# Moving the start addresses of four weight buffers in a two-layer encoder kernel

## The chip, the core and the metric

The kernel runs on one core of one Trainium2 chip. The metric is device microseconds (us) of the whole program. TensorE (PE in the profile) multiplies matrices: a weight load (PEld) puts a 128x128 stationary operand into the array, and a matmul streams a moving operand of up to 512 columns through it into PSUM. VectorE (DVE), ScalarE (ACT) and GpSimd (POOL) work on SBUF and PSUM, and DMA queues move data between HBM and SBUF.

## The reference

Two encoder layers work on 256 tokens of width 1024, in float32:

```python
for l in range(DEPTH):          # DEPTH = 2
    x = mixer_sublayer(x, norm1_g[l], w_in[l], ..., w_out[l], tables)
    x = channel_sublayer(x, norm2_g[l], w_gate_up[l], conv_w[l], conv_b[l], w_down[l])
...
def channel_sublayer(x, n2, w_gu, cw, cb, w_dn):
    h = rms_norm(x, n2)
    g, u = jnp.split(h @ w_gu, 2, axis=-1)
    g = depthwise_conv_centred(g, cw, cb)
    return x + (jax.nn.gelu(g, approximate=False) * u) @ w_dn
```

The mixer projects the normed input to 2560 columns, runs three kinds of attention on 16 heads of width 64 (a neighbourhood, a dilated and a grouped one), norms each kind's output, and projects back to 1024. The channel part widens to 2 x 2816 columns and comes back to 1024.

## The kernel before

**Precision by splitting.** Every large product is made of operands that are split in two: a rounded part ("hi") and what the rounding left ("lo"), both in a 4-byte float type that TensorE takes at one column a cycle. A product is then three matmuls, hi by hi, hi by lo and lo by hi (`mm3`, lines 708 to 711). In the gate and up products (`half_up`, lines 1337 to 1372) the weights are the stationary operand and the activations, hi and lo side by side in one tile `hT`, are the moving one: eight matmuls of 512 columns with the weights' hi part ("wide" below), then eight of 256 columns with their lo part ("narrow"), and that twice for a unit of 256 weight columns. In the projections, the output projections and the down product (`down`, lines 1424 to 1444), the weights are the moving operand, 384, 256 or 512 columns at a time.

**The weight buffers.** All weights pass through the pool `wp` in units of up to 2048 columns (8 KB a partition). A DMA on SP's queue loads a unit into one of four `raw` buffers (`load`, lines 644 to 674). ACT copies it, rounded, into one of two `hi` buffers, and DVE writes raw minus hi into one of two `lo` buffers, 384 to 1024 columns an instruction (`split`, lines 676 to 695). Units take the two slots of each kind in turn. The split runs two units ahead of the matmuls (`AHEAD`, line 42). The output projection's weights of layer 1 are split early, during layer 0, and parked in HBM (`keep`, lines 628 to 642); four of those six units come back by DMA from POOL's queue straight into hi and lo buffers (lines 687 to 689), the other two into buffers of the pool `act`.

**The order of the work.** Every call is first recorded. A planner (`Plan.order`, lines 323 to 465) puts the instructions of all engines in one order from a table of costs, and `emit` (lines 467 to 472) issues them in that order; therefore all instructions carry line 472 in the profile, and groups are told apart by the names of their tiles. In the feed-forward part, one step is a gate unit, a down unit and an up unit: 64 matmuls of the gate and up products and 24 of the down product, 22 steps in the two layers.

**Where buffers get their address.** `Slots.place` (lines 175 to 181) asks the real pool for one tile per slot when the slot is first used, and `View.bind` (lines 146 to 163) cuts the operand of an instruction out of it. The planner doesn't see addresses. In the built program of before, all tiles of `wp` and all large ones of `act` begin at a multiple of 512 bytes in each partition (hi 0 at 69632, lo 0 at 77824, hi 1 at 102400, lo 1 at 110592). Within them, matmul operands begin at multiples of 512 bytes, too. Two kinds of tiles differ: `const_x`, the residual stream, begins 384 bytes past a multiple of 512; and in the value tiles `const_v` (line 598, rows of 13 or 5 heads of 256 bytes) every second weight load begins 256 bytes past one.

Of the kernel before, what the change touches and what calls it, by code (L numbers as in the profile page):

```python
# [37 lines left out]
BANK = 512  # L38
# [124 lines left out]
        return ap  # L163


class Slots:


# [6 lines left out]
    def place(self, t):  # L175
        if t.slot not in self.places:
            shape = list(t.shape) if self.dram else [P, BANK if self.psum else self.cols]
            self.places[t.slot] = self.pool.real.tile(
                shape, self.dtype, tag=f"{self.tag}{t.slot}", name=f"{self.pool.name}_{self.tag}{t.slot}", bufs=1
            )  # L180
        return self.places[t.slot]


# [55 lines left out]
class Plan:  # L239
# [83 lines left out]
    def order(self):  # L323
# [79 lines left out]
        while len(done) < len(ops):  # L403
# [24 lines left out]
            for t in o.tiles:  # L428
                if t.slot is None:
                    s = t.pool  # L430
                    s.given += 1
                    place = min(s.free)
                    s.free.remove(place)
                    t.since, t.slot = taken_at(place[0], ""), place[1]
# [1117 lines left out]
```

## Time and profile before

| what | value |
|---|---|
| time, median of 3 runs | 605.19 us (604.93 to 605.29) |
| the profiled execution's own time | 605.52 us |
| its span, first to last instruction | 603.7 us |
| PE busy, PEld busy | 598.0 us (99%), 526.5 us (87%) |
| DVE, ACT, POOL busy | 485.0, 428.6, 81.0 us |
| granted TensorE clock | 1.00 all along, the 2.4 GHz level |
| DMA | 121.44 MB, mean 201 GB/s |

A matmul's bar in the trace overlaps the next one's, as matmuls are pipelined and their ends modelled. What a matmul costs is the distance from its start to the next one's start, and "pace" below means that distance.

### The profile page before, as it was taken

How to read it: one execution, taken by the hardware profiler on the slowest of the kernel's cores; microseconds unless marked ns; L12 is line 12 of the kernel's file. 1: busy time of each engine (PE TensorE's matmuls, PEld its weight loads, DVE VectorE, ACT ScalarE, POOL GpSimd, SP SyncE). 2: the span in 40 equal slices, each digit the busy share in tenths (PEclk: the TensorE clock that was granted, in tenths of full speed). 3: DMA queues.
4: the chain of work that ended last, by engine and by line, in shares of the span. 5: the costliest groups of instructions: out<-in, count | busy, mean ns of one | idle time of the engine just before them, and what ended most of it. 6: DMA issues, size and time to landing. Idle time of an engine off the chain costs nothing.

```text
span 603.7 us, 9899 instructions
## 1 busy us (share of the span) xinstructions
PE 598.0 (99%) x3496; PEld 526.5 (87%) x3496; DVE 485.0 (80%) x995; ACT 428.6 (71%) x1065; POOL 81.0 (13%) x130
## 2 busy tenths in 40 slices
PE   8999999999999999999999999999999999999997
PEld 7999898888888888888899989888888888888886
DVE  4899988997788988888777898777977777777775
ACT  6889999696566767666688899676766556665661
POOL 2733030102400000000023214421000000000000
PEclk9999999999999999999999999999999999999999
DMA  8993313567588898989454726844465556555601
GB/s 281 292 334 108 106 36 108 181 202 241 174 239 295 280 347 301 331 291 318 153 148 157 254 71 244 280 177 140 140 208 203 171 186 210 175 178 206 197 12 69
DMA packets 85217, 121.44 MB, mean 201 GB/s; under 512 B 9880, under 2 KB 69880, under 8 KB 85168
## 3 DMA queue, kind: packets, MB, share of 16 engines
q1 hardware_dynamic: 82896, 112.17, 55.9%
q0 software_dynamic: 1728, 8.39, 4.1%
q8 instruction: 27, 0.44, 0.3%
q10 hardware_dynamic: 544, 0.26, 0.2%
q14 instruction: 22, 0.18, 0.1%
HBM read 110.93 MB, written 9.88 MB: 200 GB/s over the span
## 4 chain that ended last, share of the span: by engine, by line
PE 97%; ACT 1%; DVE 1%; POOL 0%; issue 0%; DVEq 0%; POOLq 0%
PE psw_w L472 53%; PE psa_a L472 44%; ACT act_s2k L472 0%; POOL small_rstd L472 0%; ACT act_z L472 0%; DVE act_z L472 0%; ACT act_hT L472 0%; DVE wp_lo L472 0%; DVE act_sw L472 0%; POOL small_ms L472 0%; DVE const_x L472 0%; DVE act_qo L472 0%; ACT wp_hi L472 0%; POOL const_warm L472 0%; DVEq L472 0%
## 5 line engine op out<-in xcount | busy, mean ns | idle before, releaser
L472 DVE TENSOR_TENSOR wp_lo<-wp_raw,wp_hi 128x512 fp32r<-128x512 f32 (+2 forms) x332 | 231.4, 731 | 57.2 <-ACT wp_hi L472 40.3
L472 ACT CAST wp_hi<-wp_raw 128x512 fp32r<-128x512 f32 (+2 forms) x332 | 203.0, 663 | 21.6 <-PE psw_w L472 10.1
L472 PE MATMUL psw_w<-act_hT,wp_hi 128*128 128x512 f32 x704 | 179.8, 393 | 0.0
L472 PEld LDWEIGHTS psw_w<-act_hT,wp_hi 128*128 128x128 f32 x704 | 127.8, 189 | 24.2 <-DVE act_hT L472 0.6
L472 PE MATMUL psa_a<-wp_hi,act_hT 128*128 128x384 f32 (+2 forms) x448 | 112.9, 332 | 0.7 <-ACT wp_hi L472 0.7
L472 PEld LDWEIGHTS psw_w<-act_hT,wp_lo 128*128 128x128 f32 x704 | 97.7, 190 | 6.7
L472 PE MATMUL psw_w<-act_hT,wp_lo 128*128 128x256 f32 x704 | 102.2, 282 | 0.0
L472 PEld LDWEIGHTS psa_a<-wp_hi,act_hT 128*128 128x128 f32 x448 | 78.4, 189 | 3.3 <-ACT wp_hi L472 0.9
L472 PE MATMUL psa_a<-wp_lo,act_hT 128*128 128x384 f32 (+2 forms) x224 | 74.4, 334 | 0.1
L472 ACT COPY act_s2k<-psw_w 128x256 f32<-128x256 f32 x88 | 32.4, 372 | 59.4 <-PE psw_w L472 58.9
L472 PE MATMUL psa_a<-wp_lo,act_ch 128*128 128x512 f32 (+1 forms) x176 | 68.3, 388 | 0.0
L472 PE MATMUL psa_a<-wp_hi,act_ch 128*128 128x512 f32 x176 | 68.2, 388 | 0.0
L472 PE MATMUL psa_a<-wp_hi,act_cl 128*128 128x512 f32 (+1 forms) x176 | 67.5, 387 | 0.0
L472 DVE TENSOR_TENSOR act_s2k<-psw_w,act_s2k 128x256 f32<-128x256 f32 x88 | 36.6, 421 | 12.8 <-ACT act_s2k L472 12.0
L472 PEld LDWEIGHTS psa_a<-wp_lo,act_hT 128*128 128x128 f32 x224 | 42.3, 189 | 2.4 <-DVE wp_lo L472 1.1
L472 PEld LDWEIGHTS psa_a<-wp_hi,act_cl 128*128 128x128 f32 x176 | 33.1, 188 | 6.8
L472 PEld LDWEIGHTS psa_a<-wp_hi,act_ch 128*128 128x128 f32 x176 | 33.1, 188 | 6.3
L472 PEld LDWEIGHTS psa_a<-wp_lo,act_ch 128*128 128x128 f32 x176 | 33.1, 188 | 6.0
L472 DVE SCALAR_TENSOR_TENSOR act_s2k<-act_s2k,act_cw,act_s2k 128x255 f32<-128x255 f32 x88 | 36.8, 477 | 1.4 <-ACT act_s2k L472 1.3
L472 ACT ACTIVATE act_s2k<-act_s2k 128x512 f32<-128x512 f32 x22 | 13.9, 632 | 30.3 <-DVE act_s2k L472 30.2
L472 ACT ACTIVATE act_s2k<-act_s2k,act_cw 128x256 f32<-128x256 f32 x44 | 24.1, 596 | 15.3 <-DVE act_s2k L472 15.3
L472 POOL TENSOR_TENSOR small_rstd<-small_ms,const_mh 128x6 f32<-128x6 f32 (+2 forms) x26 | 30.9, 1188 | 14.2 <-DVE small_ms L472 12.6
(132 smaller groups left out, 792.0 us busy)
## 6 DMA issues: line engine op xcount, KB each, us to landing
wp_raw<-in_w_gate_up_dram SPq DMA_DIRECT2D x44, 1024.0 KB, 4.9
wp_raw<-in_w_down_dram SPq DMA_DIRECT2D x22, 1024.0 KB, 7.2
wp_raw<-in_w_in_dram SPq DMA_DIRECT2D x14, 768.0 KB, 5.2
wp_raw<-in_w_in_dram SPq DMA_DIRECT2D x8, 1024.0 KB, 6.8
wp_raw<-in_w_out_dram SPq DMA_DIRECT2D x8, 768.0 KB, 9.3
dram_khi<-act_mixT_hi SPq DMA_DIRECT2D x4, 768.0 KB, 3.6
dram_klo<-act_mixT_lo SPq DMA_DIRECT2D x4, 768.0 KB, 8.3
wp_lo<-dram_klo POOLq DMA_DIRECT2D x4, 768.0 KB, 4.7
```

The costliest lines, as they stand in the source:

```text
L472: getattr(o.engine.real, o.method)(*map(real, o.args), **{k: real(v) for k, v in o.kw.items()})
```

## The change

Four weight buffers, the two hi and the two lo slots of `wp`, get 128 more columns (512 bytes) each, and the part of them that is used begins 8, 48, 16 or 32 columns in, that is 32 bytes (hi 0), 192 (hi 1), 64 (lo 0) and 128 (lo 1). All instructions, their order and their sizes stay. Tiles that lie behind one of the four move up by 512 bytes for each, 2048 in all, so they keep their place relative to a multiple of 512. The raw buffers stay on multiples of 512.

```diff
+SHIFTS = {("hi", 0): 8, ("hi", 1): 48, ("lo", 0): 16, ("lo", 1): 32}
+
+
 class Slots:
...
     def place(self, t):
         if t.slot not in self.places:
             shape = list(t.shape) if self.dram else [P, BANK if self.psum else self.cols]
-            self.places[t.slot] = self.pool.real.tile(
+            shift = SHIFTS.get((self.tag, t.slot), 0)
+            if shift:
+                shape[1] += BANK // 4
+            place = self.pool.real.tile(
                 shape, self.dtype, tag=f"{self.tag}{t.slot}", name=f"{self.pool.name}_{self.tag}{t.slot}", bufs=1
             )
+            self.places[t.slot] = place[:, shift:] if shift else place
         return self.places[t.slot]
```

## Rows read from the trace of the kernel before

**Rows 1.** The page: busy time of PE and PEld, and the chain that ended last.

```profile
PE 598.0 (99%) x3496; PEld 526.5 (87%) x3496; DVE 485.0 (80%) x995; ACT 428.6 (71%) x1065; POOL 81.0 (13%) x130
...
PE 97%; ACT 1%; DVE 1%; POOL 0%; issue 0%; DVEq 0%; POOLq 0%
```

**Rows 2.** Waits of PE: who waited for whom, us, times, longest us.

```profile
PE psw_w L472 <- POOL const_warm L472: 1.0, 1, 1.0
PE psa_a L472 <- ACT wp_hi L472: 0.7, 1, 0.7
```

**Rows 3.** Groups of PE on the weight buffers: count, busy us, mean ns, idle us.

```profile
L472 PE MATMUL psw_w<-act_hT,wp_hi 128*128 128x512 f32 x704 | 179.8, 393 | 0.0
L472 PE MATMUL psa_a<-wp_hi,act_hT 128*128 128x384 f32 (+2 forms) x448 | 112.9, 332 | 0.7 <-ACT wp_hi L472 0.7
L472 PE MATMUL psw_w<-act_hT,wp_lo 128*128 128x256 f32 x704 | 102.2, 282 | 0.0
L472 PE MATMUL psa_a<-wp_lo,act_hT 128*128 128x384 f32 (+2 forms) x224 | 74.4, 334 | 0.1
L472 PE MATMUL psa_a<-wp_lo,act_ch 128*128 128x512 f32 (+1 forms) x176 | 68.3, 388 | 0.0
L472 PE MATMUL psa_a<-wp_hi,act_ch 128*128 128x512 f32 x176 | 68.2, 388 | 0.0
L472 PE MATMUL psa_a<-wp_hi,act_cl 128*128 128x512 f32 (+1 forms) x176 | 67.5, 387 | 0.0
```

**Rows 4.** Timeline of PE, 237.8 to 249 us: start us, us until its end, instruction.

```profile
237.81 0.40 PE L472 MATMUL psa_a<-wp_hi,act_ch 128*128 128x512 f32 x1
...
238.97 0.39 PE L472 MATMUL psa_a<-wp_hi,act_cl 128*128 128x512 f32 x1
...
243.05 0.39 PE L472 MATMUL psa_a<-wp_hi,act_cl 128*128 128x512 f32 x1
243.28 1.98 PE L472 MATMUL psw_w<-act_hT,wp_hi 128*128 128x512 f32 x8
245.09 1.12 PE L472 MATMUL psw_w<-act_hT,wp_lo 128*128 128x256 f32 x8
246.04 2.00 PE L472 MATMUL psw_w<-act_hT,wp_hi 128*128 128x512 f32 x8
247.88 1.12 PE L472 MATMUL psw_w<-act_hT,wp_lo 128*128 128x256 f32 x8
```

**Rows 5.** The chain in order of time, one step: start us, us, what.

```profile
226.82 11.15 PE psw_w L472 x64
237.97 5.47 PE psa_a L472 x24
```

**Rows 6.** Views by tile: duration ns min/median/max of matmuls whose stationary tile differs.

```profile
L472 PE MATMUL psw_w<-const_ident,const_x x64: 270/272/421, 4.7 to 417.7; 128*128 128x128 f32 x64
L472 PE MATMUL psw_w<-const_ident,act_z x60: 270/272/273, 28.6 to 379.4; 128*128 128x128 f32 x60
...
L472 PE MATMUL psw_w<-act_ch,const_v x128: 274/282/387, 55.0 to 404.8; 128*128 128x256 f32 x128
L472 PE MATMUL psw_w<-act_hT,wp_lo x704: 274/283/287, 120.4 to 588.4; 128*128 128x256 f32 x176
```

**Rows 7.** Groups of DVE and ACT that fill the buffers, from the page.

```profile
L472 DVE TENSOR_TENSOR wp_lo<-wp_raw,wp_hi 128x512 fp32r<-128x512 f32 (+2 forms) x332 | 231.4, 731 | 57.2 <-ACT wp_hi L472 40.3
L472 ACT CAST wp_hi<-wp_raw 128x512 fp32r<-128x512 f32 (+2 forms) x332 | 203.0, 663 | 21.6 <-PE psw_w L472 10.1
```

**Rows 8.** Stretch 138 to 300 us: PE, PEld, DVE, ACT, POOL busy, clock, DMA.

```profile
138.00:300.00 162.00, 162.00 (x857) 139.67 (x856) 133.79 (x227) 106.57 (x195) 11.10 (x18) 1.00 0.81 273
```

**Rows 9.** DMA issues into the moved buffers: KB each, median us to landing.

```profile
wp_lo<-dram_klo POOLq DMA_DIRECT2D x4, 768.0 KB, 4.7
wp_hi<-dram_khi POOLq DMA_DIRECT2D x4, 768.0 KB, 5.9
```

## The prediction

> **What bounds the kernel now.** I read the page first: PE is busy for 598.0 of 603.7 us, and 97% of the chain that ended last lies on PE [rows 1]. The view of PE's waits confirms it: in the whole execution PE waits twice, 1.7 us together [rows 2]. No transfer and no other engine is waited for. The time is thus the sum of the matmuls' paces, and the change can move it by two ways alone: it changes the pace of matmuls that read the moved buffers, or it slows those that fill them by so much that PE begins to wait.
>
> How many matmuls read them is in PE's groups: 704 + 448 + 704 + 224 + 3 x 176 = 2608 with hi or lo weights on either side [rows 3] (the output projections, not shown, add to that). One TensorE cycle at the granted 2.4 GHz is 0.42 ns, so **one cycle on each is 1.1 us**, 0.18% of the time. About 0.2%, 1.2 us, is what a measurement of this kernel can tell from no change. The question is whether a start address is worth a cycle or more.
>
> The timeline shows the paces. In a down unit, 18 matmuls of 512 columns take from 238.97 to 243.05 us, 0.2267 us each; but the five before them, of the same shape and from the same buffers, take 0.232 (237.81 to 238.97) [rows 4]. The up and gate products show the same: eight wide matmuls that follow wide ones take 1.81 us (243.28 to 245.09), eight that follow narrow ones 1.84 (246.04 to 247.88) [rows 4]. Nothing is waited for there. After each change of width PE thus needs some matmuls to settle. And the settled pace is not the ideal one: 512 columns at 2.4 GHz are 213.3 ns, so 13.3 ns of each go elsewhere. PE and PEld are busy at the same time for most of the span [rows 1]: the next weights are read from SBUF while the moving operand streams. If the two reads got into each other's way, both the 13.3 ns and the settling could hang on addresses. That is the only place where I can see this change act.
>
> **The change, part by part.** *Instructions and waits*: none is added, removed or moved, and no queue is passed. Each part is costed at nothing but the following.
>
> *Weights as stationary operand* (1408 matmuls on the gate and up products). No row shows a weight load that begins 32, 64, 128 or 192 bytes past a multiple of 512. The nearest do so at other places. Transposes of const_x, which begins 384 bytes past, have the same shortest and median duration as transposes of act_z, which begins on a multiple: 270 and 272 ns [rows 6]. In the attention's last product every second weight load of const_v begins 256 bytes past a multiple; shortest and median are 274 and 282 ns, against 274 and 283 for the lo weights, all of which begin on one [rows 6]. So two other starts cost nothing that shows. I take 0, from these rows.
>
> *Weights as moving operand* (1200 of the 2608). No row has a moving operand off a multiple of 512. Both ends have to come from the paces. **Below**: the shift undoes the settling. In one step that is 0.03 us for the down unit (5.47 us against 24 x 0.2267 = 5.44 [rows 4, 5]) and 0.03 for each of the three of four wide blocks that follow narrow ones, 0.12 us in all. 22 steps make 2.6 us. The steps are 22 x (11.15 + 5.47) = 366 us of the span [rows 5]; if the rest has as much, it is 2.6 x 603.7/366 = 4.3 us. **Above**: matmuls that read a moved buffer never settle, and pay 0.232 for 0.2267 us, 5 ns. Hi 0 alone begins off a multiple of 64 bytes; hi buffers serve 704 + 448 + 352 = 1504 matmuls [rows 3], of which hi 0 has half, and 752 x 5 ns = 3.8 us. Between -4.3 and +3.8 us I take 0: the nearest rows, those of the shifted weight loads, are at 0.
>
> Here a row and a rule differ. The row is that equal matmuls without a wait have two paces [rows 4]. The Trainium skill, SBUF — State Buffer, section "Who interferes with whom", says that PE reads the moving operand and the weights through two independent ports, and that PE and ACT never wait on anyone. By that rule neither pace can hang on an address, and the sum stays at 0; it leaves the two paces without an explanation, so it isn't proof. By the row taken as a collision of the reads, the sum could be -2.6 us.
>
> *Writes by ACT and DVE into the buffers*. 332 instructions each, 663 and 731 ns on average [rows 7]. From 138 to 300 us, DVE is busy 133.79 of 162 us and ACT 106.57 [rows 8]. DVE's 28.2 idle us over that stretch's 9.7 steps with 10 pieces each, 97 pieces, leave 0.29 us a piece, 40% of its duration: so much slower would each have to be before DVE sets the pace. If that cover went, each 0.1 us beyond it would cost 22 x 10 x 0.1 = 22 us. I see no reason for such a slowdown and cost it at nothing.
>
> *The eight DMAs into hi and lo*. They take 4.7 and 5.9 us [rows 9], and no wait of PE is for a transfer [rows 2]. A start 32 bytes off may cost them something; PE's work on the units before them hides it. Nothing.
>
> The sum is 0. The profiled execution took 605.52 us, its span of 603.7 and 1.8 around it; that is 0.33 over the median of 605.19, to which the forecast refers: **605.2 us**.
>
> **The rivals.** *Faster, the settling goes.* If the two paces come from weight load and moving operand reading the same part of SBUF in step, then moving one of them by 32 to 192 bytes takes them out of step. It is worth 2.6 us, up to 4.3: 602.6, at best 600.9. For it: the pace depends on what came just before, with no wait to explain it [rows 4], and all operands of before begin alike. Against it: the weight loads at 256 and 384 bytes run no faster [rows 6].
>
> *Much faster, the surcharge goes.* If the 13.3 ns on each settled matmul are collisions, and they go, 2608 x 13.3 ns = 34.7 us: 570. Against it: shifted weight loads of const_v, with their duration unchanged, should already show a part of it [rows 6].
>
> *Slower, a start inside a 64-byte piece costs a fetch.* Its place are the matmuls on hi 0, as moving operand or in the weight load; its price is the unsettled pace, 5 ns on 752 matmuls: 3.8 us, 609.0. It decides from 1.6 ns a matmul (1.2 us / 752), four cycles. For it: PE has no idle time that would cover it [rows 1]. Against it: the rows at 384 and 256 bytes, which however are multiples of 64 and can't speak for 32.
>
> *The change doesn't do what it says.* If the pool placed the larger tiles so that the used part began on a multiple of 512 again, everything would be as before: 605.2. Little speaks for it, since the cut is made within the tile.
>
> **How the numbers follow.** No effect gets 0.45 and the void change 0.02, together 0.47 for 605.2 within 1.2 us. The settling's loss gets 0.27, the surcharge's 0.03, together 0.30 for faster. The extra fetch gets 0.23, with which other losses of the same place go. Faster stands above slower because the known surcharge leaves more to win than a multiple of 32 bytes seems able to lose. The likeliest case's own range is 604.0 to 606.4. The range given reaches to the bound of the settling case, 600.9, and to the slower case, 609.0: outside are 0.03 for the large gain and a part of each side that goes past its bound, 0.2 together.
>
> **What would show it.** In the timeline of the changed kernel, right would be: settled matmuls of 512 columns at 0.2267 us, the first five after a narrow block at 0.232, a step of 11.15 + 5.47 us, PE's two waits as before, and 731 ns on average for DVE's pieces. The settling case would show blocks of eight at 1.81 us also after narrow ones. The fetch case would show steps that alternate, units in hi 0 longer than those in hi 1. I would be wrong as a whole if PE began to wait for DVE or ACT, or if paces changed in instructions that touch none of the four buffers.

## The result and the profile after

The changed kernel takes 608.33 us (607.75 to 608.96, 5 runs) against 605.19 (604.56 to 606.35, 5 runs): the ratio is 1.005, with a 95% interval of 1.0036 to 1.0065. It is **slower by 3.1 us**, half a per cent. That lies inside the range given and beyond what a measurement can tell from no change, on the side that had a chance of 0.23. The profiled execution took 608.96 us with a span of 607.2, so it is 0.6 over the median; it is compared with the profiled execution of before (605.52, span 603.7). Times of the runs below are medians of 4 to 11 executions; of the run with `hT` at 240 bytes, one execution of ten took 1200.55 us, for which no trace has a reason, and is left out.

Busy times and the chain after, from the page, answer to [rows 1]:

```profile
PE 601.1 (99%) x3496; PEld 526.0 (87%) x3496; DVE 484.3 (80%) x995; ACT 428.4 (71%) x1065; POOL 79.8 (13%) x130
...
PE 95%; DMA 2%; ACT 1%; DVE 1%; POOL 0%; issue 0%; ACTq 0%; DVEq 0%; POOLq 0%
```

PE is busy 3.1 us longer with the same 3496 matmuls; no other engine is. (None of POOL's 130 instructions reads or writes PSUM, in either trace.) The waits of PE after (us, times, longest) answer to [rows 2]:

```profile
PE psw_w L479 <- POOL const_warm L479: 1.0, 1, 1.0
PE psa_a L479 <- ACT wp_hi L479: 0.7, 1, 0.7
PE psa_a L479 <- DVE wp_lo L479: 0.5, 2, 0.2
```

So 0.5 us of waiting is new, and most of the rest has to be in the paces. The chain in order of time (start us, us, what) shows the steps, of which [rows 5] has one:

```profile
211.64 11.19 PE psw_w L479 x64
222.83 5.55 PE psa_a L479 x24
228.38 11.24 PE psw_w L479 x64
239.62 5.51 PE psa_a L479 x24
245.13 11.19 PE psw_w L479 x64
```

A gate and up pair and its down unit took 11.15 + 5.47 = 16.62 us each time [rows 5]. Now two kinds of step alternate, since three units a step go to two slots in turn: 11.24 + 5.51 = 16.75 and 11.19 + 5.55 = 16.74. That is 0.125 us more on average, and 22 steps make **2.75 us**, most of the loss. The timeline (start us, us until its end, instruction) says how, beside [rows 4]:

```profile
240.84 0.39 PE L479 MATMUL psa_a<-wp_hi,act_ch 128*128 128x512 f32 x1
...
244.28 0.39 PE L479 MATMUL psa_a<-wp_hi,act_ch 128*128 128x512 f32 x1
...
244.97 2.02 PE L479 MATMUL psw_w<-act_hT,wp_hi 128*128 128x512 f32 x8
246.83 1.11 PE L479 MATMUL psw_w<-act_hT,wp_lo 128*128 128x256 f32 x8
247.77 2.03 PE L479 MATMUL psw_w<-act_hT,wp_hi 128*128 128x512 f32 x8
249.64 1.09 PE L479 MATMUL psw_w<-act_hT,wp_lo 128*128 128x256 f32 x8
250.56 1.99 PE L479 MATMUL psw_w<-act_hT,wp_hi 128*128 128x512 f32 x8
252.39 1.11 PE L479 MATMUL psw_w<-act_hT,wp_lo 128*128 128x256 f32 x8
253.34 2.01 PE L479 MATMUL psw_w<-act_hT,wp_hi 128*128 128x512 f32 x8
255.19 1.13 PE L479 MATMUL psw_w<-act_hT,wp_lo 128*128 128x256 f32 x8
```

In this down unit, which has the buffers of slot 1 (hi 192, lo 128), the 15 matmuls from 240.84 to 244.28 take 0.2293 us each: what settled at 0.2267 [rows 4] no longer gets there. The up unit behind it has those of slot 0 (hi 32, lo 64): eight wide matmuls take 1.86 and 1.87 us, where they took 1.81 after wide ones and 1.84 after narrow ones; eight narrow ones take 0.94 and 0.92, where they took 0.95 (245.09 to 246.04). The gate unit after that, from 250.56 on, is again one of slot 1: 1.83 and 1.85 for wide blocks, 0.95 for the first narrow one. Wide matmuls lost, most of all in slot 0, and there the narrow ones won a little.

The remaining difference is at the beginning. PE's block of 39 matmuls on psa_a begins at 38.80 us before and at 39.63 after, and the chain of the profile after passes through a load of w_in into a raw buffer there. Raw buffers still begin on multiples of 512, and this is one execution against one; it isn't counted as the change's.

### The profile page after: what moved, and what is told of

Same layout as the page of the kernel before. It is cut to its first block, busy times and chain, and to the rows that moved or that the text cites. A ratio compares the mean times of both kernels' runs of the same rounds, so it can differ in the third digit from the quotient of the medians.

```text
span 607.2 us, 9899 instructions
## 1 busy us (share of the span) xinstructions
PE 601.1 (99%) x3496; PEld 526.0 (87%) x3496; DVE 484.3 (80%) x995; ACT 428.4 (71%) x1065; POOL 79.8 (13%) x130
## 4 chain that ended last, share of the span: by engine, by line
PE 95%; DMA 2%; ACT 1%; DVE 1%; POOL 0%; issue 0%; ACTq 0%; DVEq 0%; POOLq 0%
PE psw_w L479 53%; PE psa_a L479 42%; DMA wp_raw<-in_w_in_dram 2%; ACT act_s2k L479 0%; ACT wp_hi L479 0%; POOL small_rstd L479 0%; ACT act_z L479 0%; DVE act_z L479 0%; DVE wp_lo L479 0%; ACT act_hT L479 0%; DVE act_sw L479 0%; DVE const_x L479 0%; POOL small_ms L479 0%; DVE act_qo L479 0%; POOL const_warm L479 0%
```

## The experiments

The theories at the start: **relative**, the read of the weights being loaded and the read of the streaming operand get into each other's way, depending on how their starts lie to each other; **absolute**, an operand's own start costs; **placement**, the 512 to 2048 bytes by which later tiles move.

### Four runs to tell the theories apart

The room without the shift (all four tiles 512 bytes larger, used from their beginning):

```diff
+PADDED = ("hi", "lo")
...
-            shift = SHIFTS.get((self.tag, t.slot), 0)
-            if shift:
+            if self.tag in PADDED:
                 shape[1] += BANK // 4
...
-            self.places[t.slot] = place[:, shift:] if shift else place
+            self.places[t.slot] = place
```

> The four buffers get the 512 extra bytes but begin on multiples of 512 again, so that all later tiles move by 512 to 2048 bytes as in the change. Start theory (what counts is where an operand begins within 512 bytes): 605.2 us as before, within 0.6; 18 matmuls of a down unit settle at 0.2267 us. Rival, placement (the move of the later tiles makes the loss): about 608.3, as in the change.

Measured: 605.6 us, ratio to before 1.0001 (0.9992 to 1.001). Its steps in the chain:

```profile
227.01 11.15 PE psw_w L478 x64
238.16 5.47 PE psa_a L478 x24
```

They are those of before: the placement theory is out.

Hi 0 alone:

```diff
-SHIFTS = {("hi", 0): 8, ("hi", 1): 48, ("lo", 0): 16, ("lo", 1): 32}
+SHIFTS = {("hi", 0): 8}
```

> Hi 0 alone begins 32 bytes past a multiple of 512; the other three stay. In the two profiles hi 0's matmuls account for about 2.2 of the 3.5 us. If the losses of the four buffers add up: 607.4 us (606.9 to 608), and units in the other slots run as before (down units 5.47 us, eight wide matmuls after narrow ones 1.84). If the loss comes from the four starts differing among each other: under 606.

Measured: 607.63 us against 605.59, ratio 1.0036 (1.0024 to 1.0048). The chain:

```profile
210.51 11.21 PE psw_w L479 x64
221.72 5.55 PE psa_a L479 x24
227.27 11.19 PE psw_w L479 x64
238.45 5.47 PE psa_a L479 x24
```

Down units in the unmoved slot take 5.47 as before, those with hi 0 take 5.55. One buffer makes two thirds of the change's loss.

All four at 32 bytes:

```diff
-SHIFTS = {("hi", 0): 8, ("hi", 1): 48, ("lo", 0): 16, ("lo", 1): 32}
+SHIFTS = {("hi", 0): 8, ("hi", 1): 8, ("lo", 0): 8, ("lo", 1): 8}
```

> All four buffers begin 32 bytes past a multiple of 512. If a 32-byte start is the dear one for each buffer: twice hi 0's 2.2 us and something for lo, 609.5 us or more. If differing starts make the loss and a common one doesn't: under 606.

And, from the kernel before, everything behind the pool `const` at 32 bytes, the activations with the weights:

```diff
-    few_out = const.tile([P, 496], F32, tag="fo", name="few_out")[:, :1]
+    few_out = const.tile([P, 504], F32, tag="fo", name="few_out")[:, :1]
```

> From the kernel before, a spare tile ahead of the pools wp and act is 32 bytes wider, so raw, hi, lo and all tiles of act begin 32 bytes later: weights and activations keep their starts relative to each other. Relative theory (the read of the weights being loaded and that of the streaming operand collide by how their starts lie to each other): 605.2 us, settled matmuls at 0.2267 us. Absolute theory (a start off a larger multiple costs by itself): at least as slow as the kernel with all four buffers at 32, 609.5 or more.

Measured: all four at 32 take 611.62 us, ratio 1.0089 (1.0068 to 1.0111). Everything at 32 takes 605.2, ratio 0.9987 (0.9977 to 0.9996). The chain of the first:

```profile
227.34 11.24 PE psw_w L479 x64
238.58 5.60 PE psa_a L479 x24
```

and of the second:

```profile
225.84 11.15 PE psw_w L472 x64
236.99 5.47 PE psa_a L472 x24
```

In both kernels the four weight buffers begin 32 bytes past a multiple of 512. In the one, the activations don't, and a step takes 0.22 us more; in the other they do, and it takes what it took before. This tells the theories apart: **it is the weights' start relative to the activations' that counts**, not the weights' own. It also speaks against the writes of ACT, DVE and the DMAs as the cause: the hi and lo buffers that they fill begin 32 bytes past a multiple of 512 in both. In time, all four at 32 lose 6.0 us (4 executions), of which the steps' 22 x 0.22 make 4.8; the rest was not placed.

### Four runs on which distances cost

The change without its hi 0 part:

```diff
-SHIFTS = {("hi", 0): 8, ("hi", 1): 48, ("lo", 0): 16, ("lo", 1): 32}
+SHIFTS = {("hi", 1): 48, ("lo", 0): 16, ("lo", 1): 32}
```

> The change without its hi 0 part: hi 1 at 192, lo 0 at 64, lo 1 at 128 bytes, hi 0 on a multiple of 512. Theory P (starts collide modulo 64 bytes: 64, 128 and 192 are as good as 0): 605.2 to 605.6 us, settled matmuls of 512 columns at 0.2267 us in every slot. Theory Q (any relative start other than 0 within 512 bytes has its own pace): the loss that hi 0 alone doesn't explain stays, 608.3 - 607.6 + 605.4 = 606.1 us, and units in slot 1 don't settle at 0.2267.

Measured: 607.56 us against 605.37, ratio 1.0044 (1.0029 to 1.0059); more than Q's 606.1. Without hi 0's shift, the change loses about as much as hi 0 does alone, 2.2 us, and the two together make 3.1: the losses don't add up. The chain, and two starts within its first down unit, say where:

```profile
221.42 5.57 PE psa_a L479 x24
...
238.15 5.50 PE psa_a L479 x24
```

```profile
222.65 0.40 PE L479 MATMUL psa_a<-wp_hi,act_ch 128*128 128x512 f32 x1
...
226.59 0.39 PE L479 MATMUL psa_a<-wp_hi,act_cl 128*128 128x512 f32 x1
```

The unit of 5.57 us is that of slot 0. Its hi buffer is back on a multiple of 512, and only its lo buffer begins 64 bytes past one; yet the 17 matmuls from 222.65 to 226.59, two thirds of them on hi, take 0.232 us each and don't settle. With both buffers 64 bytes past, a down unit takes 5.49 us (below). So the starts of the matmuls around one count as well, not its own pair of operands alone. And it shows why the losses don't add up: in slot 0's down unit hi 0 alone costs 0.08 us (5.55), lo 0 alone 0.10 (5.57), and both together 0.08 (5.55).

The other three have one distance for all four buffers (64 bytes shown; 32 and 64 columns for 128 and 256 bytes):

```diff
-SHIFTS = {("hi", 0): 8, ("hi", 1): 48, ("lo", 0): 16, ("lo", 1): 32}
+SHIFTS = {("hi", 0): 16, ("hi", 1): 16, ("lo", 0): 16, ("lo", 1): 16}
```

> All four buffers 64 bytes past a multiple of 512. P: as before, 605.4 us, 1.81 us for eight wide matmuls after wide ones. Q: another pace than 0.2267 us; slower than before, by how much is open (32 bytes made 6 us).

> All four buffers 128 bytes past a multiple of 512. P: as before, 605.4 us. Q: another pace than 0.2267 us; if the loss falls with the distance from 0, less than with 64.

> All four buffers 256 bytes past a multiple of 512. P and, by the rows on const_v (every second weight load 256 past, no difference), Q as well: as before, 605.4 us. If the pace still changes, those rows were read wrongly.

Measured: 64 bytes 604.76 us (0.9993; 0.9983 to 1.0002), 128 bytes 610.41 (1.009; 1.0075 to 1.0105), 256 bytes 605.21 (1.0000; 0.9991 to 1.001). The chains, 64 bytes:

```profile
226.25 11.10 PE psw_w L479 x64
237.35 5.49 PE psa_a L479 x24
```

128 bytes:

```profile
228.37 11.25 PE psw_w L479 x64
239.62 5.57 PE psa_a L479 x24
```

and 256 bytes:

```profile
226.24 11.15 PE psw_w L479 x64
237.39 5.47 PE psa_a L479 x24
```

256 bytes are as good as none. 128 bytes lose 5 us, so it isn't multiples of 64 that are safe: P is out. And 64 bytes look harmless in the time, but not in the timeline:

```profile
242.68 2.03 PE L479 MATMUL psw_w<-act_hT,wp_hi 128*128 128x512 f32 x8
244.54 1.07 PE L479 MATMUL psw_w<-act_hT,wp_lo 128*128 128x256 f32 x8
245.46 2.02 PE L479 MATMUL psw_w<-act_hT,wp_hi 128*128 128x512 f32 x8
247.32 1.07 PE L479 MATMUL psw_w<-act_hT,wp_lo 128*128 128x256 f32 x8
248.23 2.02 PE L479 MATMUL psw_w<-act_hT,wp_hi 128*128 128x512 f32 x8
```

Wide blocks take 1.86 us, never 1.81; narrow ones 0.92 and 0.91 instead of 0.95. Both paces moved, in opposite directions: Q was right of the paces, and wrong in expecting a slower kernel. The gate and up pair wins 0.05 us, the down unit loses 0.02. A kernel that took this distance in the gate and up products alone should therefore be faster than before.

### Four runs that move the activations instead

The gate and up products read `hT` beside the weights, the down unit doesn't. (The projections at the beginning of a layer read it, too: it is the stationary operand of their 672 matmuls, the second and fourth line of [rows 3].) Moving `hT` by 192 bytes puts the weights 64 past it, modulo 256:

```diff
-SHIFTS = {("hi", 0): 8, ("hi", 1): 48, ("lo", 0): 16, ("lo", 1): 32}
+SHIFTS = {("hT", 0): 48}
```

> The four weight buffers stay on multiples of 512; instead the activations' tile hT begins 192 bytes past one, which is 64 before the next multiple of 256. Relative theory with a period of 256 bytes: the gate and up products run as in the kernel with all four buffers at 64 (11.10 us a pair, narrow blocks 0.91 to 0.92 us, wide ones after narrow 1.86), while the down units, which don't read hT, run as before (5.47). 22 x (16.62 - 16.57) = 1.1 us off 605.3: 604.2, a fifth of a per cent faster. Absolute theory (weights' own starts count): 11.15 and 5.47, 605.3 us.

Measured: 604.12 us against 605.38, ratio 0.9981 (0.9972 to 0.999). The chain:

```profile
226.26 11.11 PE psw_w L479 x64
237.37 5.46 PE psa_a L479 x24
```

and PE's timeline, in a gate and up pair:

```profile
245.45 2.02 PE L479 MATMUL psw_w<-act_hT,wp_hi 128*128 128x512 f32 x8
247.31 1.07 PE L479 MATMUL psw_w<-act_hT,wp_lo 128*128 128x256 f32 x8
248.22 2.02 PE L479 MATMUL psw_w<-act_hT,wp_hi 128*128 128x512 f32 x8
```

Blocks of 1.86 and 0.91 us, as with all four weight buffers at 64, though no weight buffer was moved; down units as before. The time came out within 0.1 us of the 604.2 that the theory gave. For the three other distances the edit differs in the number of columns alone (16, 40, 60).

> hT 64 bytes past a multiple of 512, weights unmoved: the weight loads begin 64 before the moving operand, 192 modulo 256. If the sign doesn't count: gate and up as with all four at 64, 11.10 us a pair. If it does: another pace; hi 1 at 192 in the changed kernel gave wide blocks of 1.85 us, so 11.15 or more. Down units 5.47 in both cases.

> hT 160 bytes past a multiple of 512, relative start 96 modulo 256. If only multiples of 64 do well (0, 64, 256 did; 32 didn't, but neither did 128): a pair of gate and up takes 11.24 us or more, as with all four at 32; 607 us. If the loss falls off with the distance from 0 and 256: between.

> hT 240 bytes past a multiple of 512, relative start 16 modulo 256. If the reads meet in pieces of 32 bytes or more: nearly as before, 11.15 us a pair. If 16 bytes already take them out of step: a pace of its own, nearer to the 11.24 us of 32 bytes than to 11.15.

Measured, as steps of the chain, for hT at 64 bytes (weights 192 past it):

```profile
225.82 11.09 PE psw_w L479 x64
236.91 5.47 PE psa_a L479 x24
```

at 160 bytes (96 past):

```profile
227.12 11.26 PE psw_w L479 x64
238.38 5.45 PE psa_a L479 x24
```

and at 240 bytes (16 past):

```profile
226.06 11.22 PE psw_w L479 x64
237.28 5.45 PE psa_a L479 x24
```

The times are 603.26 us (ratio 0.9965; 0.9952 to 0.9979), 608.41 (1.0047; 1.0033 to 1.0061) and 606.27 (1.0018; 1.0007 to 1.0029). 192 isn't 64 with the sign turned: it has blocks of its own and the shortest pair of all, 11.09 us, where I had expected 11.15 or more. 96 loses what was expected, a little more in time (3.0 us, of which the steps make 22 x 0.09 = 2.0). With 192 the steps win 22 x 0.06 = 1.3 of the 2.1 us. Whether the remainders lie in the projections was not looked into. At 16 bytes the pace already differs, with 11.22 us near to what 32 bytes cost. The trace of the run at 160 bytes records a granted clock of 0.95 throughout, its three other executions 1.00; its time of 608.17 us lies among theirs (607.51 to 608.68), and its down units took 5.45 us as elsewhere, so neither shows it.

**A kernel that beats both** is thus the one of before with `hT` 64 bytes further on: 2.1 us less than before, 5 less than the changed kernel.

## Why the prediction was right, and where it wasn't

**The bound: right.** PE set the time before and after, its waits stayed small (1.7 and 2.2 us), and the loss went through the paces of matmuls. The place was named, too: the weight load and the moving operand that stream at the same time, and how their starts lie to each other.

**The sum: wrong.** The step that failed is the one under *weights as moving operand* that took 0 between -4.3 and +3.8 us, "the nearest rows, those of the shifted weight loads, are at 0", and the same 0 for the stationary weights. These rows were poor witnesses. The weight loads of const_v begin 256 bytes past, and 256 bytes are the distance that the run with all four buffers there shows to be none at all. The transposes of const_x begin 384 past, 128 modulo 256, where the run with all four at 128 lost 5 us; but I compared durations there, whose ends are modelled, of matmuls of 128 columns, and not their pace in a stream of wide ones. "No difference in the nearest row" held for the row and not for the quantity. In place of the 0 stand 2.75 us in the steps, of 3.1 measured: 1.4 in the gate and up products, where the weights are stationary (11.15 to 11.215 us on average), and 1.3 in the down products, where they move (5.47 to 5.53). The few tenths left were not placed.

**The slower rival: near in its number, wrong in its mechanism.** It gave 3.8 us and 609.0, with hi 0 as its place. Hi 0 alone makes 2.0 us, and steps do alternate. But a start inside a 64-byte piece isn't the cause: with everything at 32 bytes nothing is lost, and at 128, a multiple of 64, 5 us are. Its count was mixed, too: of the 752 matmuls on hi 0, 352 have it as the stationary operand, the part that had been costed at 0. The bound took a good price, the kernel's own unsettled pace of 0.232 us, near which the down units in fact ran (0.229 to 0.233). That the time stayed under 609.0 is luck all the same: other distances on the same buffers take 610.4 (all at 128) and 611.6 us (all at 32), and the likeliest case, 604.0 to 606.4, was missed.

**The faster rivals: the idea right, the sign open.** The pace does hang on how the two starts lie to each other, and moving one does pay at 192 bytes (2.1 us) and at 64 in the gate and up products (1.1 us). The four distances of the change are a mixture in which hi 0's 32 bytes and the rest lose more than the narrow blocks win. Operands that all begin alike, against which the rival argued, are among the better arrangements, not the worst.

**The rule weighed there.** All four buffers at 32 bytes and everything at 32 bytes have the same starts of the weights within 512 bytes and different ones of the activations, and are 0.22 us apart in each step (the 512 to 2048 bytes by which tiles moved cost nothing in the run without the shift). The Trainium skill, SBUF — State Buffer, section "Who interferes with whom", has PE's two read ports independent of each other; taken as "neither pace can hang on an address", as I took it, it disagrees with that number, and the measurement decides.

**Costed at nothing and found so:** the writes by ACT and DVE, 664 and 736 ns on average against 663 and 731 [rows 7], and the loads into lo and hi buffers, 4.8 and 6.0 us to landing against 4.7 and 5.9 [rows 9].

**What stays open** is the mechanism inside: why 64 bytes quicken narrow matmuls and slow wide ones, why 192 differs from 64, and how one matmul's starts reach the next ones' paces. That the two reads from SBUF get into each other's way is argued, not shown; shown are the dependence on the distance and the repeat at 256. Distances other than 16, 32, 64, 96, 128, 192 and 256 weren't tried, nor different ones for hi and lo beside a moved `hT`.

## What to carry to other kernels

Where PE is the bound and streams matmuls without a wait, look at the distance between their starts rather than at the bars: if equal matmuls have several paces, the starts of the operands in SBUF are worth a run each. What counts is the stationary operand's start relative to the moving one's, modulo 256 bytes here, and that of the matmuls around it; one tile can be moved for the products that read it without touching the others (`hT` left the down units at 5.45 to 5.47 us). The sum over a step is what to compare, since one pace can win what the other loses. A row that shows no difference clears only the distance that it has: check that it isn't a multiple of the period before taking it for the case at hand.

## What the hardware showed that I had not expected

- Matmuls of the same shape, fed without any wait, run at paces from 0.2267 to 0.233 us (down unit, everything at 32 bytes, settled, against all four weight buffers at 32: 5.60 us / 24) by the relative start of their operands alone.
- The period is 256 bytes to the precision of the trace: 11.15 and 5.47 us at distance 0 and at 256, and blocks of 1.86 and 0.91 us with the weights 64 past `hT` (all four at 64) and 192 before it (`hT` at 192).
- The distance of 64 bytes takes eight narrow matmuls from 0.95 to 0.91 us and eight wide ones that follow narrow ones from 1.84 to 1.86.
- A matmul whose own operands all begin on multiples of 512 can lose its settled pace by the start of its neighbours: 0.232 us on hi 0 beside a lo 0 that begins 64 bytes past.
